# Turning the sample's 64 rows as full blocks of 128 outside the attention

## The chip, the cores and the metric

The kernel runs on one core of one Trainium2 chip. The metric is device time in microseconds (us), from the start to the end of one execution; the median of three runs of the kernel before is 1720.67 us (1717.54 to 1723.04).

## The reference, cut to what matters

One layer of a streaming encoder, for a prompt of 1024 tokens and a sample of 64 tokens with 128 cached keys, in float32. Both pass the same layer:

```python
z = rmsnorm(x, norm_mix) @ w_in                 # 1024 -> qa ka va qi ki wi qb kb vb ga gb
qa, ka, qi, ki = rmsnorm per head (not qi), rotary on the first 16 of 64 columns
qb, kb = rmsnorm per head
isc = sum_h wi[h] * relu(qi[h] @ ki.T)          # indexer: the best 256 keys (48 for the sample)
oa = softmax(qa @ ka.T / 8 over the chosen keys) @ va
ob = softmax(qb @ kb.T / 8 + bias over a band of 9 chunks) @ vb
x = x + (sigmoid(ga) * (oa @ w_o_a) + sigmoid(gb) * (ob @ w_o_b)) @ w_out
y = x + square(relu(rmsnorm(x, norm_ffn) @ w_up)) @ w_down
```

The outputs are y for prompt and sample and the new keys and values.

## The kernel before, in words

The 1024 prompt tokens are eight blocks of 128 rows (i = 0 to 7); the 64 rows of the sample are block 8 (i = NT), with rows = 64. Wherever a matmul needs tokens along the columns, a block is turned by TensorE: `nc.tensor.transpose` with the identity, four 128-column pieces of a block into one PSUM bank, then ScalarE copies the bank out rounded to float32r (the high half) and DVE subtracts that from the bank (the low half). All products are made of high and low halves by `three` (lines 154 to 156) or `two` (lines 162 and 163).

There are five places that turn a block of the sample outside the attention:

- `to_columns` (line 181), the normalised input xg, two groups of four, called by `stage_columns`;
- `index_keys` (line 241), the indexer's key kd, one transposition;
- `stage_scores` (line 349), the indexer's queries qd, two groups of four, one for each four heads;
- `rows_to_dram` (line 411), the projected t of kb, qb, ka and qa (the values vb and va are not turned), one group of four each, called by `keep` in `project_heads`;
- `ffn_columns` (line 930), the normalised input xg of the feed-forward part, two groups of four.

For i < 8 they turn 128 x 128; for the sample 64 x 128, with the identity cut to 64 x 64, and the four results stand side by side in 4 x 64 columns of the bank:

```python
nc.tensor.transpose(ps[:, q * rows:(q + 1) * rows], xg[:rows, k * P:(k + 1) * P],
                    ident[:rows, :rows])
```

The tiles come from rotating buffers: xg has 2 (line 167), kd 3, qd 2, t 3. DVE writes xg (line 172); ScalarE, DVE and POOL (rotary, lines 220 to 223, gains, line 461) write the others. POOL also makes the low halves of most weights (`split`, line 148), in whose queue everything on POOL stands in order. In the attention, `weigh_sample` (line 736) already turns the sample in full blocks.

Except in a few blocks (`issue_after`), the order of the instructions on an engine is not written by hand: the framework places them by a simulated clock, in the order in which they become ready there.

Of the kernel before, what the change touches and what calls it, by code (L numbers as in the profile page):

```python
# [44 lines left out]
def kernel(  # L45
# [58 lines left out]
    def ptile():  # L104
        return bank("pt")
# [16 lines left out]
    def copy(out, in_):  # L122
        return nc.scalar.activation(out, in_, AF.Copy)  # L123
# [42 lines left out]
    def rms_rows(pool, xt, rows, gain):  # L166
        xg = pool.tile([P, D], F32, tag="xg", name="xg", bufs=2)
        junk = pool.tile([P, D], mybir.dt.bfloat16, tag="junk", name="junk", bufs=1)
        ss = pool.tile([P, 8], F32, tag="ss", name="ss", bufs=3)
        nc.scalar.activation(junk[:rows], xt[:rows], AF.Square, accum_out=ss[:rows, 0:1])  # L170
        rs = rstd(pool, ss, D, rows, 1)
        last["scaled"] = nc.vector.scalar_tensor_tensor(xg[:rows], xt[:rows], rs[:rows, 0:1], gain[:rows],
                                                        op0=ALU.mult, op1=ALU.mult)
        return xg

    def to_columns(xg, rows, dst, c0):
        for j in range(2):
            ps = ptile()
            for q in range(4):
                k = 4 * j + q  # L180
                nc.tensor.transpose(ps[:, q * rows:(q + 1) * rows], xg[:rows, k * P:(k + 1) * P],
                                    ident[:rows, :rows])
            v = ps[:, :4 * rows].rearrange("p (q r) -> p q r", q=4)
            hi = dst[:, 4 * j:4 * j + 4, 0, c0:c0 + rows]
            last["turned"] = copy(hi, v)
            nc.vector.tensor_sub(dst[:, 4 * j:4 * j + 4, 1, c0:c0 + rows], v, hi)
# [52 lines left out]
    def index_keys(kd, rows, c0):  # L239
        ps = ptile()  # L240
        nc.tensor.transpose(ps[:, :rows], kd[:rows].rearrange("p a d -> p (a d)"), ident[:rows, :rows])
        copy(kih[:, c0:c0 + rows], ps[:, :rows])
        nc.vector.tensor_sub(kil[:, c0:c0 + rows], ps[:, :rows], kih[:, c0:c0 + rows])
# [51 lines left out]
    def stage_keys(i):  # L295
        rows = P if i < NT else TS
        z1, _ = project(i, acc(), parts["keys"], 584 - SPLIT)
        kd = ix.tile([P, 2, HD], F32, tag="kd", name="kd", bufs=3)
        ss = ix.tile([P, 8], F32, tag="ss", name="ss", bufs=3)
# [11 lines left out]
        qd = ix.tile([P, H, 2, HD], F32, tag="qd", name="qd", bufs=2)  # L311
        copy(qd[:rows, 5:8, 0, :], z1[:rows, :192].rearrange("p (h d) -> p h d", d=HD))
# [17 lines left out]
    def stage_scores(i, between={}):  # L330
# [15 lines left out]
        for j in range(2):  # L346
            ps = ptile()
            for q in range(4):
                nc.tensor.transpose(ps[:, q * rows:(q + 1) * rows],
                                    qd[:rows, 4 * j + q].rearrange("p a d -> p (a d)"), ident[:rows, :rows])  # L350
            v = ps[:, :4 * rows].rearrange("p (q r) -> p q r", q=4)
# [56 lines left out]
    def rows_to_dram(t, rows, dst, c0, gain=None):  # L408
        ps = ptile()
        for j in range(4):  # L410
            nc.tensor.transpose(ps[:, j * rows:(j + 1) * rows], t[:rows, j * P:(j + 1) * P], ident[:rows, :rows])
        v = ps[:, :4 * rows].rearrange("p (j r) -> p j r", j=4)
# [22 lines left out]
    def project_heads():  # L435
        for nm, c0, gn, roped in (("vb", C_VB, None, False), ("kb", C_KB, "kb", False), ("qb", C_QB, "qb", False),
# [9 lines left out]
            for i in range(NT + 1):  # L446
                z, rows = project(i, wide_acc(), ws, 512)
                t = pj.tile([P, 512], F32, tag="t", name="t", bufs=3)
                if gn is None:
# [469 lines left out]
    def ffn_columns(i):  # L919
# [6 lines left out]
        for j in range(2):  # L926
            ps = ptile()
            for q in range(4):
                k = 4 * j + q
                nc.tensor.transpose(ps[:, q * rows:(q + 1) * rows], xg[:rows, k * P:(k + 1) * P],  # L930
                                    ident[:rows, :rows])
            v = ps[:, :4 * rows].rearrange("p (q r) -> p q r", q=4)
# [447 lines left out]
```

## Time and profile before

| | us |
|---|---|
| median of three runs | 1720.67 (1717.54 to 1723.04) |
| the profiled execution | 1716.99 |
| its span, first to last instruction | 1715.2 |
| TensorE (PE) busy | 1693.6 |
| weight loads (PEld) busy | 1548.0 |
| DVE (VectorE) busy | 1200.7 |
| ACT (ScalarE) busy | 957.4 |
| POOL (GpSimd) busy | 454.9 |

The profile is of one execution, taken by the hardware profiler. PE is TensorE's matmul side, PEld its weight load, which runs beside it; SP issues most DMAs. In a timeline a line is one instruction, or several alike in a row (x4), with its start and duration in us, the engine, the line of the kernel, what it writes and reads, and the tile of TensorE's array as rows\*columns (64\*128 is a matmul with 64 rows of weights). Where the engine sat idle before an instruction, the bracket says how long and who ended it. Matmuls are pipelined, so the distance between two starts tells what one costs, not its recorded duration.

### The profile page before, as it was taken

To read this page: it belongs to the slowest core of one execution; us is meant where nothing else is said; L and a number is where in the kernel's file an instruction comes from. 1 tells how busy PE (TensorE), PEld (TensorE's weight loads), DVE (VectorE), ACT (ScalarE), POOL (GpSimd) and SP (SyncE) were. 2 spreads that over 40 slices of the span, in tenths; PEclk is the share of its full clock that TensorE was granted. 3 is DMA by queue.
4 is the path that set the end of the run, shared out by engine and by line. 5 is a ranking of instruction groups with operands and counts; after the bars stand their busy time and mean duration, and the time that the engine had idled before them with its cause. 6 is when DMAs were issued, how large, how long until landed. Compare 5 with 4: busy or idle time off the path is not lost. (4 is left out here: it accounts for less than half of the span.)

```text
span 1715.2 us, 30888 instructions
## 1 busy us (share of the span) xinstructions
PE 1693.6 (99%) x10552; PEld 1548.0 (90%) x10552; DVE 1200.7 (70%) x2760; ACT 957.4 (56%) x1984; POOL 454.9 (27%) x550
## 2 busy tenths in 40 slices
PE   8999999999999999999999999999999999999999
PEld 6878878778999999999999999999999978788887
DVE  6775799864957777773454446765687668877787
ACT  5784889762267777775443446544454356343430
POOL 2242441434343343342344434000000001112112
PEclk9999999999999999999999999999999999999999
DMA  5022466483488877745545459555565599565643
GB/s 176 10 77 105 147 187 172 136 267 95 138 204 204 209 170 170 171 113 161 166 146 169 158 163 297 180 175 176 176 215 192 188 304 311 173 206 150 191 127 105
DMA packets 277422, 295.01 MB, mean 172 GB/s; under 512 B 39889, under 2 KB 201937, under 8 KB 277265
## 3 DMA queue, kind: packets, MB, share of 16 engines
q1 hardware_dynamic: 248144, 257.50, 51.6%
q10 hardware_dynamic: 29120, 35.53, 5.9%
q8 instruction: 84, 1.38, 0.3%
q14 instruction: 74, 0.60, 0.1%
HBM read 199.85 MB, written 93.08 MB: 171 GB/s over the span
## 5 line engine op out<-in xcount | busy, mean ns | idle before, releaser
L155 PE MATMUL x<-lo,hi 128*128 128x512 f32 (+1 forms) x436 | 169.2, 388 | 0.3 <-DVE lo L146 0.3
L156 PE MATMUL x<-hi,lo 128*128 128x512 f32 (+1 forms) x436 | 167.6, 389 | 0.0
L154 PE MATMUL x<-hi 128*128 128x512 f32 (+1 forms) x436 | 164.9, 390 | 1.2 <-DVE q_P L1254 1.2
L148 POOL TENSOR_TENSOR lo<-wr,hi 128x512 fp32r<-128x512 f32 x12 | 31.6, 2635 | 482.7 <-ACT hi L123 482.7
L148 POOL TENSOR_TENSOR lo<-raw,hi 128x512 fp32r<-128x512 f32 x88 | 118.2, 1352 | 143.4 <-ACT hi L123 142.7
L123 ACT ACTIVATE hi<-raw 128x512 fp32r<-128x512 f32 x104 | 64.2, 626 | 90.9 <-PE acc L155 21.0
L539 ACT ACTIVATE nth<-work,cand 128x768 bf16<-128x768 f32 (+2 forms) x93 | 96.7, 1040 | 25.8 <-DVE cand L556 18.3
L155 PE MATMUL wide<-wlo,xnT 128*128 128x512 f32 x256 | 101.2, 398 | 0.0
L154 PE MATMUL wide<-whi,xnT 128*128 128x512 f32 x256 | 100.4, 398 | 0.7 <-ACT whi L123 0.7
L156 PE MATMUL wide<-whi,xnT 128*128 128x512 f32 x256 | 101.1, 397 | 0.0
L154 PEld LDWEIGHTS x<-hi 128*128 128x128 f32 x436 | 81.8, 188 | 19.0 <-DVE q_P L1254 1.6
L155 PEld LDWEIGHTS x<-lo,hi 128*128 128x128 f32 x436 | 81.9, 188 | 18.3 <-DVE lo L146 0.7
L156 PEld LDWEIGHTS x<-hi,lo 128*128 128x128 f32 x436 | 81.8, 188 | 17.8
L726 DVE TENSOR_TENSOR pl<-pt,ph 128x512 fp32r<-128x512 f32 (+2 forms) x152 | 90.9, 614 | 9.4 <-ACT ph L123 9.1
L154 PE MATMUL acc<-xnT,hi 128*128 128x384 f32 (+1 forms) x288 | 95.6, 332 | 0.0
L155 PE MATMUL acc<-xnT,hi 128*128 128x384 f32 (+1 forms) x288 | 94.5, 328 | 0.0
L156 PE MATMUL acc<-xnT,lo 128*128 128x384 f32 (+1 forms) x288 | 94.4, 328 | 0.0
L146 DVE TENSOR_TENSOR lo<-hr,hi 128x512 fp32r<-128x512 f32 x108 | 80.7, 748 | 19.4 <-ACT hi L123 19.4
L123 ACT ACTIVATE ph<-pt 128x512 fp32r<-128x512 f32 (+3 forms) x168 | 79.7, 514 | 25.3 <-PE pt L714 16.3
L701 POOL TENSOR_SCALAR mw<-mw,sm 128x640 f32<-128x640 f32 (+1 forms) x64 | 56.6, 885 | 133.8 <-DVE sm L700 131.3
L148 POOL TENSOR_TENSOR wlo<-wraw,whi 128x512 fp32r<-128x512 f32 x40 | 52.5, 1318 | 106.7 <-ACT whi L123 97.4
L123 ACT ACTIVATE hi<-wr 128x512 fp32r<-128x512 f32 x60 | 37.9, 631 | 75.5 <-issue 52.6
(679 smaller groups left out, 5999.3 us busy)
## 6 DMA issues: line engine op xcount, KB each, us to landing
hr<-h SPq DMA_DIRECT2D x108, 256.0 KB, 3.5
wr<-in_w_down_dram SPq DMA_DIRECT2D x76, 256.0 KB, 3.9
wraw<-in_w_in_dram SPq DMA_DIRECT2D x56, 256.0 KB, 2.7
h<-h ACTq DMA_DIRECT2D x32, 272.0 KB, 2.1
raw<-in_w_out_dram SPq DMA_DIRECT2D x32, 256.0 KB, 3.0
raw<-in_w_up_dram SPq DMA_DIRECT2D x32, 256.0 KB, 3.4
out_dram<-t SPq DMA_DIRECT2D x24, 256.0 KB, 2.5
g_dram<-gate SPq DMA_DIRECT2D x32, 192.0 KB, 2.8
```

The lines of the kernel that those rows point to most:

```text
L123: return nc.scalar.activation(out, in_, AF.Copy)
L146: last["lo"] = nc.vector.tensor_sub(lo, raw, hi)
L148: nc.gpsimd.tensor_sub(lo, raw, hi)
L154: nc.tensor.matmul(out, sh, mh, start=(opens and i == 0), stop=False, skip_group_check=resumes)
L155: nc.tensor.matmul(out, sh, ml, start=False, stop=False, skip_group_check=resumes)
L156: last = nc.tensor.matmul(out, sl, mh, start=False, stop=(closes and i == n - 1), skip_group_check=resumes)
L539: nc.scalar.activation(sign[:, :w.shape[1]], w, AF.Sign, bias=against, scale=-1.0, accum_out=col(cnt, j))
L701: nc.gpsimd.tensor_scalar(m[:rows, :n], m[:rows, :n], sm[:rows, 6:7], 1.0, op0=ALU.mult, op1=ALU.mult)
L726: nc.vector.tensor_sub(pl[:kr, a:b], ps[:kr, a:b], ph[:kr, a:b])
```

## The change

Each of the five places gives whole 128-row tiles to one function, `turn_rows`, which turns 128 x 128 with the full identity and hands back the first `rows` columns of each result. For the sample, the upper 64 partitions of the tile are set to zero by a memset on GpSimd (`fill`); for full blocks `fill` does nothing. There are eight such memsets: xg twice (in `rms_rows` for the first norm and again for the feed-forward part), kd, qd, and t for kb, qb, ka and qa. The evictions read the first 64 columns of every 128. The diff, cut where places repeat:

```diff
         ss = pool.tile([P, 8], F32, tag="ss", name="ss", bufs=3)
+        fill(xg, rows)
         nc.scalar.activation(junk[:rows], xt[:rows], AF.Square, accum_out=ss[:rows, 0:1])
...
+    def fill(t, rows):
+
+        if rows < P:
+            nc.gpsimd.memset(t[rows:], 0.0)
+
+    def turn_rows(srcs, rows):
+        ps = ptile()
+        for q, t in enumerate(srcs):
+            nc.tensor.transpose(ps[:, q * P:(q + 1) * P], t, ident)
+        return ps.rearrange("p (q r) -> p q r", q=4)[:, :, :rows]
+
     def to_columns(xg, rows, dst, c0):
         for j in range(2):
-            ps = ptile()
-            for q in range(4):
-                k = 4 * j + q
-                nc.tensor.transpose(ps[:, q * rows:(q + 1) * rows], xg[:rows, k * P:(k + 1) * P],
-                                    ident[:rows, :rows])
-            v = ps[:, :4 * rows].rearrange("p (q r) -> p q r", q=4)
+            v = turn_rows([xg[:, k * P:(k + 1) * P] for k in range(4 * j, 4 * j + 4)], rows)
...
     def index_keys(kd, rows, c0):
         ps = ptile()
-        nc.tensor.transpose(ps[:, :rows], kd[:rows].rearrange("p a d -> p (a d)"), ident[:rows, :rows])
+        nc.tensor.transpose(ps[:, :P], kd.rearrange("p a d -> p (a d)"), ident)
...
         kd = ix.tile([P, 2, HD], F32, tag="kd", name="kd", bufs=3)
+        fill(kd, rows)
...
         qd = ix.tile([P, H, 2, HD], F32, tag="qd", name="qd", bufs=2)
+        fill(qd, rows)
...
                 t = pj.tile([P, 512], F32, tag="t", name="t", bufs=3)
+                if nm[0] != "v":
+                    fill(t, rows)
```

`stage_scores`, `rows_to_dram` and `ffn_columns` call `turn_rows` in the same way as `to_columns` does.

## Rows read from the trace of the kernel before

**Rows 1.** The page: busy time of each engine, share of the span, instructions.

```profile
PE 1693.6 (99%) x10552; PEld 1548.0 (90%) x10552; DVE 1200.7 (70%) x2760; ACT 957.4 (56%) x1984; POOL 454.9 (27%) x550
```

**Rows 2.** Busy time by stage: stretch, length, engines' busy us, clock, DMA; first, sum.

```profile
0.00:92.00 92.00, 82.70 (x541) 72.22 (x542) 68.79 (x182) 60.69 (x152) 22.96 (x81) 0.98 0.28 87
...
960.00:1078.00 118.00, 117.41 (x979) 116.50 (x978) 65.93 (x121) 66.99 (x127) 49.45 (x35) 1.00 0.69 212
...
sum 1715.00, PE 1693.57 PEld 1547.97 DVE 1200.69 ACT 957.38 POOL 454.86; mean PE 211.70 PEld 193.50 DVE 150.09 ACT 119.67 POOL 56.86
```

**Rows 3.** Groups of TensorE by shape: count, busy us, mean ns, idle us before.

```profile
L411 PE MATMUL pt<-ident,t 64*128 64x64 f32 x16 | 1.8, 230 | 1.6 <-DVE pair L417 1.4 <-DVE cand L571 0.2
L930 PE MATMUL pt<-ident,xg 64*128 64x64 f32 x8 | 0.9, 235 | 0.0
L181 PE MATMUL pt<-ident,xg 64*128 64x64 f32 x8 | 0.9, 235 | 0.0
L349 PE MATMUL pt<-ident,qd 64*128 64x64 f32 x8 | 0.7, 228 | 0.0
...
L241 PE MATMUL pt<-ident,kd 64*128 64x64 f32 x1 | 0.2, 246 | 0.2 <-DVE qiT L354 0.2
```

**Rows 4.** Timeline of TensorE around the sample's first group at line 930.

```profile
1002.51 0.28 PE L155 MATMUL acc<-lo,mT 128*128 128x256 f32 x1
1002.72 0.46 PE L930 MATMUL pt<-ident,xg 64*128 64x64 f32 x4
1003.11 0.39 PE L156 MATMUL acc<-hi,mT 128*128 128x256 f32 x1
1003.34 0.28 PE L154 MATMUL acc<-hi,mT 128*128 128x256 f32 x1
```

**Rows 5.** Timeline of TensorE around a full block's group at line 930.

```profile
997.77 0.28 PE L154 MATMUL acc<-hi,mT 128*128 128x256 f32 x1
997.89 0.60 PE L930 MATMUL pt<-ident,xg 128*128 128x128 f32 x4
998.24 0.37 PE L155 MATMUL acc<-lo,mT 128*128 128x256 f32 x1
998.45 0.28 PE L156 MATMUL acc<-hi,mT 128*128 128x256 f32 x1
```

**Rows 6.** Timeline of TensorE: eight half transpositions, line 349; eight full ones, line 411.

```profile
116.84 0.70 PE L349 MATMUL pt<-ident,qd 64*128 64x64 f32 x8
117.48 0.44 PE L162 MATMUL s<-kih,qiT 128*128 128x384 f32 x1
...
427.56 1.04 PE L411 MATMUL pt<-ident,t 128*128 128x128 f32 x8
428.35 0.48 PE L162 MATMUL acc<-whi,xsT 128*128 128x512 f32 x1
```

**Rows 7.** Timeline of TensorE at the sample's group of kb, line 411.

```profile
243.75 0.43 PE L411 MATMUL pt<-ident,t 64*128 64x64 f32 x4 [1.43 <-DVE pair L417]
```

**Rows 8.** TensorE's waits: for whom, us in total, times, longest.

```profile
PE pt L411 <- DVE pair L417: 1.4, 1, 1.4
...
PE wide L154 <- ACT whi L123: 0.7, 1, 0.7
```

**Rows 9.** Groups of POOL by shape: memsets of 64 partitions.

```profile
L616 POOL MEMSET vhl<- 64x128 f32 x16 | 3.2, 199 | 4.1 <-PE po L744 3.3 <-PE s L162 0.9
...
L371 POOL MEMSET work<- 64x64 f32 x6 | 0.9, 148 | 12.8 <-DVE work L366 12.8
```

**Rows 10.** Timeline of all engines at a load of vhl: its two halves.

```profile
630.85 0.93 SPq L617 DMA_DIRECT2D vhl<-v_a  x1
...
631.35 0.20 POOL L616 MEMSET vhl<- 64x128 f32 x1
```

**Rows 11.** Timeline of all engines before the sample's groups at line 930.

```profile
991.76 6.11 POOL L148 TENSOR_TENSOR lo<-raw,hi 128x512 fp32r<-128x512 f32 x4 [5.45 <-ACT hi L123]
...
993.64 1.73 DVE L172 SCALAR_TENSOR_TENSOR xg<-x,rs,g_ffn 64x1024 f32<-64x1024 f32 x1 [2.33 <-PE pt L930]
```

**Rows 12.** The page's costliest groups: such a split on POOL, mean ns.

```profile
L148 POOL TENSOR_TENSOR lo<-raw,hi 128x512 fp32r<-128x512 f32 x88 | 118.2, 1352 | 143.4 <-ACT hi L123 142.7
```

More of the change, by code (lines that the diff above doesn't have):

```diff
@@ L346, in stage_scores @@
         for j in range(2):
[L347 to L351, printed above, removed]
+            v = turn_rows([qd[:, h].rearrange("p a d -> p (a d)") for h in range(4 * j, 4 * j + 4)], rows)
             dst = qiT[:, 4 * j:4 * j + 4, :rows]
@@ L408, in rows_to_dram @@
     def rows_to_dram(t, rows, dst, c0, gain=None):
[L409 to L412, printed above, removed]
+        v = turn_rows([t[:, j * P:(j + 1) * P] for j in range(4)], rows)
         both = pj.tile([P, TP], F32R, tag="pair", name="pair", bufs=3).rearrange("p (z j t) -> p z j t", z=2, j=4)
@@ L926, in ffn_columns @@
         for j in range(2):
[L927 to L932, printed above, removed]
+            v = turn_rows([xg[:, k * P:(k + 1) * P] for k in range(4 * j, 4 * j + 4)], rows)
             copy(raw[:, 4 * j:4 * j + 4, :rows], v)
```

## The prediction

> **What bounds the kernel now.** I read the busy times of the page first, then the busy time by stage, then the shapes of TensorE's instructions, and last the timeline around the transpositions that the change touches. TensorE is busy for 1693.6 of 1715.2 us [rows 1]; of the 21.4 us in which it is idle, 9.3 lie in the first 92 us [rows 2], so from there to the end 12.1 us are all that any better order could give back. The granted clock is 1.00 after the start [rows 2]: the upper of the two levels, 2.4 GHz, throughout, and nothing here rests on the clock. An edit can therefore move the time by changing what TensorE itself does, or by making it wait.
>
> The change touches one form alone, the transpositions that TensorE's records show as 64\*128. There are 41: 16 at line 411, eight each at lines 181, 349 and 930, one at line 241 [rows 3]. Their own mean, 228 to 246 ns, is longer than the distance from one to the next, since matmuls overlap, and so tells nothing of what the change is worth; the starts of the matmuls around them do.
>
> **The change part by part.**
>
> *A group of four.* Around the sample's first group at line 930, the last ordinary matmul before it starts at 1002.51 and the second after it at 1003.34: 0.83 us [rows 4]. Around a full group of four between the same 256-column matmuls these are 997.77 and 998.45: 0.68 us [rows 5]. So a group of four full transpositions takes 0.15 us less of TensorE than one of four half ones. The reason stands in the same rows: the half group begins 0.21 us after its neighbour where the full one begins after 0.12 us, and the second matmul after it follows 0.23 us after the first, against 0.21. Weights are not loaded ahead into or out of the half group. The four of the half group with their exit take 0.39 us, the full ones 0.35.
>
> *More than four.* Eight half ones, first start to the next matmul, take 117.48 − 116.84 = 0.64 us, eight full ones 428.35 − 427.56 = 0.79 us [rows 6]. Against the groups of four, the four more cost 0.25 us as halves (62 ns each) and 0.44 us as full ones (110 ns each). A full transposition is thus dearer by 48 ns; the saving is in the two ends of a group, and at line 349, where the eight stand in one piece, the change loses: 0.15 − 4 x 0.048 = −0.04 us.
>
> One rule would price that otherwise: the Trainium skill ("TensorE: Matmul & The Clock Gate", section "Back-to-back issue gap") gives 134 cycles for 128 columns and about 60 for 64 or fewer, by which the wider one would be dearer by 31 ns (an estimate at 2.4 GHz) and a group of four would save 0.22 us instead of 0.15. The rows' 48 ns decide.
>
> *The sum on TensorE.* Two groups at line 930: 0.30 us. Line 411: four groups of four, of which three begin behind a wait (the longest, 1.43 us, ends at 243.75 [rows 7]); behind a wait there is no weight load to be ahead with, so I take 0 for these (0 to 0.15 each) and 0.15 for the fourth. Line 181: 0.15 for the first group; the second is followed at once by another transposition, 0 (0 to 0.15). Line 241: a single one between waits, 0 (0 to 0.15). Line 349: −0.04. Together 0.56 us; with every zero at its upper end 1.31.
>
> *How much of it reaches the end.* What is saved before 243.75 us only lengthens the 1.43 us in which TensorE waits there for DVE, which was then working through the threshold search; so 0.26 us of it goes. The group at line 411 that saves 0.15 is followed by a wait for ScalarE of 0.7 us [rows 8], and I count it as gone too. The 0.30 us of line 930 are followed by waits as well, but in a stage in which every engine works on what TensorE has just made; I take them as kept. So: 0.30 us saved, between 0 and 1.31.
>
> *The zeros.* Eight memsets of the upper 64 partitions are added on POOL: 1024 elements a partition for the two xg tiles and for qd, 128 for kd, 512 for the t of the four heads that are turned. A memset of 64x64 takes 148 ns and one of 64x128 takes 199 [rows 9], so 0.80 ns for each further element: 0.92 us for 1024 (three), 0.51 for 512 (four), 0.20 for kd, 5.0 us together. POOL is busy for 27% of the span [rows 1]. That the written halves don't wait for one another is seen in the attention: the DMA that writes the upper 64 partitions of vhl is issued at 630.85, ahead of the memset of its lower 64 at 631.35 [rows 10]. So the memset need not hold ScalarE or DVE; it holds what is behind it in POOL's queue, and the transposition, which now waits for POOL too, and behind that all of TensorE.
>
> The tightest place is line 930. There POOL makes the low halves of the next weights, four in 6.11 us from 991.76, and the last ends at 997.87 [rows 11]; TensorE's first matmul after the group that ends at 998.24 [rows 5] uses that one, so 0.37 us are to spare. The buffer that the sample's xg takes comes free with block 2's last transposition, for which DVE waited when it begins to write it at 993.64 [rows 11], in the middle of these four. A memset put there delays TensorE by at most 0.92 − 0.37 = 0.55 us if all four splits stay as long as they are. Four at their usual 1.35 us would take 5.4 us instead of 6.11 [rows 11, 12], so some of it falls into time now lost beside DVE. I take 0.30 us; the ends are 0 and the hold worked out under the slower rival. At the other seven I take 0: POOL waits for work for long stretches around them and the splits there are ahead; the end is their 4.1 us. The evictions of the turned rows read four runs of 64 instead of one run of 256, the same element count, off TensorE's path: 0, with 0.1 us either way as bound for lack of a row.
>
> *The sum.* −0.30 + 0.30 = 0.0 us. The profiled execution took 1716.99 us, 1.79 around its span, and stays there; the median of the runs shown is 3.7 us above it at 1720.67, and the forecast is told against that: **1720.7 us**.
>
> **The rivals.**
>
> *Faster by another order.* The order of the instructions is not written by hand over most of the kernel: a framework places them by a simulated clock, in which eight new instructions and 41 wider ones can shift what follows. For it speaks that nothing pins the order outside a few blocks; against it that from 92 us on only 12.1 us of idle time are there to be won [rows 2], spread over many waits of 1.4 us and less [rows 8]. If half went, with the 0.56 us saved in full: 1720.7 − 6.6 = 1714.1 us.
>
> *Slower, by POOL's queue.* One mechanism: the memset is put ahead of weight splits and stands there until its buffer is free. At line 930, if it is first of all, POOL is held from 991.76 to 993.64, then writes for 0.92 us: the splits come 2.8 us late, 2.4 us beyond the 0.37 to spare. At line 411 the t buffer comes free only when an earlier t has been written out; if each of the four memsets holds POOL for 1 us beyond what the splits have to spare, with its own 0.51 us, that is 6.0 us. Together 8.4: 1729.1 us. It decides where the hold is longer than what the splits have to spare. For it speaks the tight place [rows 11]; against it that an order made by simulated readiness does not put an instruction where it would wait long, and that none of TensorE's longest waits is for a split of POOL [rows 8].
>
> That the change doesn't do what it says I rule out: all five places that make the 64\*128 form are in the diff.
>
> **How the numbers follow.** About 0.3% (5.2 us) is what a measurement of this kernel can tell from no change; its three runs alone lie between 1717.54 and 1723.04. The forecast, no change beyond that, has 0.79: its own bounds, −1.3 and about +2.7 us, stay within it. Faster by over 0.3% needs the first rival at nearly its full price: 0.09. Slower by over 0.3% needs the second at most of its price, or a worse order: 0.12. The range takes the scatter of the runs, 3.1 below and 2.4 above the median, and adds the bounds of the sum, 1.3 below and the 2.4 us of the hold at line 930 above: 1716.3 to 1725.5.
>
> **What would show it right or wrong.** After the change no 64\*128 form is left and 41 more full transpositions stand in TensorE's groups; around the sample's groups at line 930 the stretch reads 0.68 us instead of 0.83. The memsets read 0.9, 0.5 and 0.2 us. The three waits behind which savings vanish are still there, a little longer. TensorE's busy time falls by no more than 1.3 us. I am wrong if TensorE shows a new wait for POOL of over 1 us, at the low halves behind a memset or at a turned group; if the memset of qd or t delays ScalarE's write of the lower half; or if the stages behind 1078 us, which the change does not touch, become longer or shorter by microseconds through another order.

## The result, and the profile after

The kernel after takes 1731.36 us (median of six runs, 1727.55 to 1736.49), the kernel before beside it 1719.87 us (six runs, 1717.54 to 1723.04): a ratio of 1.0071, 95% interval [1.0057, 1.0086]. It is slower by 0.7%, some 11 us, and lies above the whole predicted range. The profiled execution took 1727.55 us with a span of 1725.8, so 10.6 us more span than the one of before; that difference is what the trace has to explain.

The page's busy times, which answer to [rows 1]:

```profile
PE 1695.3 (98%) x10552; PEld 1549.8 (90%) x10552; DVE 1207.8 (70%) x2760; ACT 956.9 (55%) x1984; POOL 458.2 (27%) x558
```

TensorE is busy 1.7 us longer, though the change was to save it 0.6; the rest of the 10.6 us is time in which it waits. DVE is busy 7.1 us longer although it has as many instructions as before. POOL has its eight memsets more and is busy 3.3 us longer.

The two things that the change itself does came out as they were priced. POOL's groups by shape hold the memsets (count, busy us, mean ns):

```profile
L180 POOL MEMSET t<- 64x512 f32 x4 | 2.1, 522 | 1.2 <-POOL wlo L148 1.0
L180 POOL MEMSET xg<- 64x1024 f32 x2 | 1.9, 948 | 0.1
L180 POOL MEMSET qd<- 64x1024 f32 x1 | 1.0, 987 | 0.6 <-PE pt L185 0.6
...
L180 POOL MEMSET kd<- 64x128 f32 x1 | 0.2, 201 | 1.5 <-issue 1.5
```

And TensorE's timeline around the sample's group in the feed-forward part, now four full transpositions (all turns have line 185):

```profile
1012.29 0.28 PE L155 MATMUL acc<-lo,mT 128*128 128x256 f32 x1
1012.41 0.60 PE L185 MATMUL pt<-ident,xg 128*128 128x128 f32 x4
1012.77 0.37 PE L156 MATMUL acc<-hi,mT 128*128 128x256 f32 x1
1012.97 0.28 PE L154 MATMUL acc<-hi,mT 128*128 128x256 f32 x1
```

1012.97 − 1012.29 = 0.68 us, where the half group took 0.83 [rows 4]. So the loss is not in what was changed. Cutting the span at the stages (first matmul of the heads, of the attention, and so on; busy time of PE, PEld, DVE, ACT, POOL, then clock and DMA) finds it. The heads stage, in which the projections of the heads and the threshold search run side by side (DVE and ScalarE find, one bit a step, the score that the chosen keys must reach), after:

```profile
163.20:489.40 326.20, 316.74 (x1512) 263.75 (x1511) 260.42 (x704) 202.47 (x394) 119.59 (x147) 0.99 0.53 157
```

The same stage before:

```profile
163.00:480.00 317.00, 314.68 (x1511) 262.56 (x1510) 250.90 (x702) 202.29 (x394) 120.58 (x143) 1.00 0.54 160
```

Of the 10.6 us, 9.2 are lost between 163 and 489 us: TensorE is idle there for 9.5 us instead of 2.3, and busy for 2.1 us longer. The stages behind it differ by 1.3 us and less (the up product most, 343.2 against 341.9). The whole of DVE's excess stands there too (260.42 against 250.90). TensorE's waits in this stage (us in total, times, longest):

```profile
PE pt L185 <- DVE pair L419: 5.0, 2, 4.2
PE pt L185 <- POOL t L230: 2.1, 1, 2.1
PE wide L155 <- DVE wlo L146: 1.2, 1, 1.2
PE pt L185 <- POOL t L465: 0.9, 1, 0.9
```

Before, the longest wait of this kind was the 1.43 us of [rows 7]. The 4.2 us are the piece to follow. They stand in TensorE's timeline:

```profile
243.48 0.40 PE L155 MATMUL wide<-wlo,xnT 128*128 128x512 f32 x1
248.05 1.09 PE L185 MATMUL pt<-ident,t 128*128 128x128 f32 x4 [4.17 <-DVE pair L419]
248.79 0.78 PE L156 MATMUL wide<-whi,xnT 128*128 128x512 f32 x1
```

and they are dearer than they look, as the windows around them show (the first pair of numbers in a row is TensorE's busy time, the first after the engines the granted clock):

```profile
240.00:244.00 4.00, 2.94 (x14) 1.81 (x12) 3.84 (x5) 0.81 (x3) 3.13 (x4) 1.00 0.59 191
244.00:248.00 4.00, 0.00 (x0) 0.00 (x0) 3.83 (x9) 2.73 (x6) 1.14 (x1) 0.97 0.08 25
248.00:252.00 4.00, 3.95 (x13) 3.37 (x14) 2.41 (x8) 3.25 (x7) 1.27 (x1) 0.60 0.86 222
```

TensorE does nothing from 244 to 248, and in the 4 us after that the granted clock averages 0.60, mostly its lower level (0.5, 1.2 GHz): 4 x (1 − 0.60) = 1.6 us more. That is most of the 2.1 us by which it is busy longer. So this place costs 4.17 − 1.43 + 1.6 = 4.3 us, about half of the 9.2; the rest is the other waits of the list, which no run here follows one by one.

What did TensorE wait for? The group is the sample's, in kb. The turned groups take two banks by turns, so it goes into the bank of kb's block 6, which was turned at 235.61 and is emptied in two steps, ScalarE's copy and DVE's subtraction at line 419. That subtraction comes only at 247.21, 11.6 us after the turn (before: turned at 234.51, subtracted at 242.92, 8.4 us). DVE's timeline up to it:

```profile
239.38 1.17 DVE L139 TENSOR_TENSOR nt<-nt,ms 64x8 f32<-64x8 f32 x1
240.58 1.20 DVE L140 SCALAR_TENSOR_TENSOR rs<-nt,r 64x8 f32<-64x8 f32 x1
...
242.67 1.35 DVE L568 COPY_PREDICATED bits<-ok,cand 128x6 int32<-128x6 int32 x1
244.05 1.12 DVE L560 TENSOR_SCALAR cand<-bits 128x6 int32<-128x6 int32 x1
...
247.21 0.69 DVE L419 TENSOR_TENSOR pair<-pt,pair 128x512 fp32r<-128x512 f32 x1
```

DVE is not idle; four operations on six or eight elements a partition take 4.84 us in front of the subtraction, where others of their kind take 0.15 to 0.17 each. ScalarE's copy is late too, behind a search step that waits for the last of the four:

```profile
246.20 0.57 ACT L123 ACTIVATE pair<-pt 128x512 fp32r<-128x512 f32 x1
```

POOL's timeline in the same stretch says why:

```profile
239.24 1.29 POOL L148 TENSOR_TENSOR wlo<-wraw,whi 128x512 fp32r<-128x512 f32 x1 [3.12 <-ACT whi L123]
240.49 1.27 POOL L465 TENSOR_TENSOR t<-t,g_kb 128x512 f32<-128x512 f32 x1
242.64 1.29 POOL L465 TENSOR_TENSOR t<-t,g_kb 64x512 f32<-64x512 f32 x1 [0.87 <-DVE ok L567]
243.89 1.25 POOL L148 TENSOR_TENSOR wlo<-wraw,whi 128x512 fp32r<-128x512 f32 x1
```

Each long operation of DVE begins just after one of POOL and ends with it: 239.38 + 1.17 = 240.55 against 240.53, 240.58 + 1.20 = 241.78 against 241.76. In the kernel before, DVE has two such operations between the same turn and the same subtraction, 2.49 us instead of 4.84:

```profile
237.68 1.26 DVE L563 TENSOR_TENSOR ok<-cnt,lim 128x6 int32<-128x6 f32 x1
...
238.97 1.23 DVE L564 COPY_PREDICATED bits<-ok,cand 128x6 int32<-128x6 int32 x1
...
242.92 0.69 DVE L417 TENSOR_TENSOR pair<-pt,pair 128x512 fp32r<-128x512 f32 x1
```

The instructions are the same; their order is not. Compared engine by engine, the two programs differ in about 50 places on ScalarE, 53 on DVE and 22 on POOL (eight of these the new memsets). On ScalarE and DVE most of them lie between the point where the sample's qd is turned and the end of the heads stage; in the attention and in the last stage there are none. So the theory: **the longer transpositions shift the simulated clock, it places the rest in another order, and in that order more of DVE's small operations meet POOL's.** (Over the whole heads stage 31 small operations of DVE last over 0.4 us, and 28 in the kernel before.) The rivals: the work itself (wider turns in TensorE's queue, zeros in POOL's), or one of the five places.

### The profile page after: what moved, and what is told of

Same layout as the page of the kernel before. It is cut to its first block, busy times and chain, and to the rows that moved or that the text cites. A ratio compares the mean times of both kernels' runs of the same rounds, so it can differ in the third digit from the quotient of the medians.

```text
span 1725.8 us, 30897 instructions
## 1 busy us (share of the span) xinstructions
PE 1695.3 (98%) x10552; PEld 1549.8 (90%) x10552; DVE 1207.8 (70%) x2760; ACT 956.9 (55%) x1984; POOL 458.2 (27%) x558
## 4 chain that ended last, share of the span: by engine, by line
PE 70%; DMA 3%; DVE 2%; issue 2%; POOL 1%; ACT 1%; SPq 0%; ACTq 0%; POOLq 0%; DVEq 0%
PE acc L154 6%; PE acc L155 6%; PE acc L156 6%; PE x L156 5%; PE x L155 5%; PE x L154 5%; PE pt L718 3%; PE po L734 2%; PE s L162 2%; PE pe L156 2%; PE pg L156 2%; PE pe L154 2%; PE pe L155 2%; PE pg L154 2%; PE pg L155 2%; PE s L163 2%
## 5 line engine op out<-in xcount | busy, mean ns | idle before, releaser
L148 POOL TENSOR_TENSOR lo<-wr,hi 128x512 fp32r<-128x512 f32 x12 | 25.9, 2160 | 485.1 <-ACT hi L123 485.1
L123 ACT ACTIVATE hi<-raw 128x512 fp32r<-128x512 f32 x104 | 64.2, 626 | 96.5 <-PE acc L155 20.8
L543 ACT ACTIVATE nth<-work,cand 128x768 bf16<-128x768 f32 (+2 forms) x93 | 96.7, 1040 | 27.2 <-DVE cand L560 20.8
L146 DVE TENSOR_TENSOR lo<-hr,hi 128x512 fp32r<-128x512 f32 x108 | 80.5, 747 | 20.9 <-ACT hi L123 20.8
```

Source lines behind the costliest of these rows:

```text
L146: last["lo"] = nc.vector.tensor_sub(lo, raw, hi)
L148: nc.gpsimd.tensor_sub(lo, raw, hi)
L543: nc.scalar.activation(sign[:, :w.shape[1]], w, AF.Sign, bias=against, scale=-1.0, accum_out=col(cnt, j))
```

## The experiments

"Heads stage" is the stretch from its first matmul to the first of the attention (before 317.0 us with 2.3 us of TensorE idle, after 326.2 and 9.5); "wait" is TensorE's wait ahead of the sample's group of kb, at 243 to 254 us (before 1.43, after 4.17). All ratios are to the kernel before on the same chip.

| run | us | ratio [95%] | heads stage, idle | wait |
|---|---|---|---|---|
| e1 zeros alone | 1721.78 | 1.0013 [0.9999, 1.0026] | 317.8, 1.8 | 1.82 |
| e2 heads alone | 1724.21 | 1.0029 [1.0015, 1.0043] | 318.7, 4.1 | 1.77 |
| e3 indexer alone | 1723.96 | 1.0028 [1.0015, 1.0041] | 322.0, 4.0 | 2.72 |
| e4 feed-forward alone | 1719.15 | 0.9998 [0.9982, 1.0013] | 317.8, 1.9 | 1.72 |
| e5 queries twice | 1727.11 | 1.0033 [1.0021, 1.0046] | 322.2, 4.0 | 2.70 |
| e6 full rows, old order | 1721.83 | 1.0011 [0.9998, 1.0023] | 317.6, 1.7 | 1.74 |
| e7 all but queries | 1726.88 | 1.0036 [1.0018, 1.0054] | 322.7, 6.1 | 1.96 |
| e8 all twice | 1727.27 | 1.0039 [1.0027, 1.0050] | 323.9, 4.6 | 2.66 |
| e9 change and six more | 1725.83 | 1.0030 [1.0016, 1.0044] | 320.1, 4.0 | 2.00 |
| e10 one step pinned | 1733.68 | 1.0091 [1.0075, 1.0108] | 327.6, 9.1 | 4.17 |
| e11 half rows, late order | 1727.54 | 1.0055 [1.0039, 1.0071] | 325.6, 7.3 | 2.59 |
| e12 change and eight more | 1732.27 | 1.0077 [1.0061, 1.0092] | 329.2, 9.0 | 2.77 |
| e13 eviction first | 1731.06 | 1.0058 [1.0046, 1.0071] | 324.3, 7.6 | 1.08 |
| e14 gains on DVE | 1725.53 | 1.0027 [1.0013, 1.0042] | 319.6, 2.8 | none |
| e15 before, gains on DVE | 1722.73 | 1.0010 [0.9999, 1.0020] | 318.2, 2.3 | none |

### One part at a time (e1 to e4)

Four kernels do one part of the change each. e1 has all eight memsets, but turns half rows. e2 to e4 turn full rows, with their zeros, in one part: the projected heads (`rows_to_dram`); the first norm, the key and the queries of the indexer (`to_columns`, `index_keys`, `stage_scores`); and the feed-forward part. The other places keep the old turn:

```diff
+    def turn_half(srcs, rows):
+        ps = ptile()
+        for q, t in enumerate(srcs):
+            nc.tensor.transpose(ps[:, q * rows:(q + 1) * rows], t[:rows], ident[:rows, :rows])
+        return ps[:, :4 * rows].rearrange("p (q r) -> p q r", q=4)
```

> The eight memsets are there, every transposition stays at 64 rows. Laid beside the kernel before, the static order of the engines' queues is all but the same (18 places differ on TensorE, 7 on DVE, against 63 and 53 in the changed kernel). Order theory (the 11.5 us come from another order of the queues between 160 and 470 us): within 0.2% of before, 1717 to 1723 us, TensorE idle about 18 to 20 us, threshold search 188 us from first to last step. Zeros theory (the memsets in POOL's queue hold the splits or the turned groups): slower by 6 us or more, with new waits of TensorE for POOL.

> Only the groups of kb, qb, ka and qa are turned as 128 rows, with their four memsets; the other places stay as before. Place theory (the loss is made directly at the turned groups of the heads, where TensorE waits 4.2 and 2.1 us in the changed kernel): slower by 6 to 11 us, with these waits in it. Order theory: the order differs from before in 70 places but little is moved (312 TensorE rows against 1406), so the time is nearer to before than to the changed kernel: slower by 0 to 5 us, search 187 to 192 us.

> Only the sample's turns before 120 us (xg of the first norm, kd, qd) are of 128 rows, with their three memsets; the groups of the heads and of the feed-forward part stay as before. Place theory and zeros theory: no loss, within 0.2% of before, since what stands in the heads is what stood there before. Order theory: the order of the queues behind them is that of the changed kernel more than that of before (1360 TensorE rows moved against before, 475 against the changed one), so slower by 5 to 12 us, between 160 and 470 us, where this kernel executes the same instructions as before.

> Only the feed-forward part's two groups are of 128 rows, with one memset. All theories: within 0.2% of before. By the prediction's own sum 0.3 us less on TensorE in the two groups (0.68 us instead of 0.83 around each) and up to 0.6 us of a later split.

The zeros alone and the feed-forward part alone can't be told from no change (their intervals include 1). The heads and the indexer cost 0.29% and 0.28%, as ratios to the kernel before. Their sum, 0.57%, is less than the 0.71% of the whole, but the more telling point is where e3 loses. Its edits are done by 163 us, before the heads stage begins, and still its heads stage is 5.0 us longer than before, with the same kind of wait (TensorE's waits, e3):

```profile
PE pt L192 <- DVE pair L426: 3.4, 2, 2.7
```

Work that was over 80 us earlier can't hold an eviction at 245 us; its shadow on the order can. (In time e3 lost 4.6 us, a little under the 5 to 12 expected.) Most of the 5.0 us is the clock behind the wait: TensorE is busy for 318.0 us in that stage instead of 314.7, and idle for 1.7 us more. e2 loses in another way: its heads stage is only 1.7 us longer, and in its profiled execution the attention (354.6 us, before 351.3) and the last stage (346.2, before 343.0) are longer too; more of that below.

### The same shift without the change (e5, e8), the change without the shift (e6, e7)

e5 is the kernel before with each of the sample's eight half transpositions of qd done twice: no zeros, no full rows. Through the heads stage its instructions stand in the order of e3 on ScalarE and on DVE, one by one.

```diff
-                nc.tensor.transpose(ps[:, q * rows:(q + 1) * rows],
-                                    qd[:rows, 4 * j + q].rearrange("p a d -> p (a d)"), ident[:rows, :rows])
+                for _ in range(1 if i < NT else 2):
+                    nc.tensor.transpose(ps[:, q * rows:(q + 1) * rows],
+                                        qd[:rows, 4 * j + q].rearrange("p a d -> p (a d)"), ident[:rows, :rows])
```

e8 doubles the sample's transpositions at all five places in this way. e6 is the whole change without the queries and the projected heads, the two parts that move most of the order; e7 is without the queries alone:

```diff
-        fill(qd, rows)
...
-            v = turn_rows([qd[:, h].rearrange("p a d -> p (a d)") for h in range(4 * j, 4 * j + 4)], rows)
+            v = turn_half([qd[:, h].rearrange("p a d -> p (a d)") for h in range(4 * j, 4 * j + 4)], rows)
```

> The kernel before, with the sample's eight half transpositions of the indexer's queries made twice (8 more of 62 ns; no zeros, no full rows anywhere). The queues of ACT, DVE and POOL come out in the order of the run with the indexer's turns alone, but for its three memsets. Order theory: slower by 2 to 7 us as that run was (0.28%), lost between 220 and 490 us. A theory in which full rows or zeros themselves cost: at most the 0.5 us that the eight repeats take on TensorE, within 0.1% of before.

> Full rows and zeros for xg of the first norm, kd and xg of the feed-forward part; the queries and the heads are turned as before. The order of the queues stays nearly that of before (9 places differ on TensorE, 7 on DVE). Order theory: within 0.15% of before, and by the prediction's sum up to 0.5 us faster. Theory that full rows or zeros cost: slower by 0.2% or more.

> The changed kernel with the queries alone turned as before: 33 of the 41 transpositions are full and seven of the eight memsets are there. Its order is nearer to before (422 TensorE rows moved) than to the changed kernel (1179). Order theory: slower by 2 to 7 us, like the run with the heads alone, not by 11. If instead the loss goes with the number of full transpositions and zeros: slower by 8 to 11 us.

> The kernel before, with all 41 half transpositions of the sample made twice (41 more of 62 ns, 2.5 us of TensorE if all counted; no zeros, no full rows). The order of ACT, DVE and POOL in the heads is near that of the changed kernel (82 ACT rows and 193 DVE rows differ, against 301 and 398 from before). Order theory: slower by 5 to 14 us, of which at most 2.5 us are the repeats, with waits of TensorE of over 2 us at turned groups between 220 and 370 us. Otherwise: slower by 2.5 us at most.

e5 is as slow as e3, and its heads stage agrees within 0.2 us (322.2 and 322.0), as do its waits (e5):

```profile
PE pt L412 <- DVE pair L418: 3.7, 2, 2.7
```

So what e3 loses needs neither zeros nor full rows. e6, with zeros and full rows in the first norm, the key and the feed-forward part but nearly the old order, has the heads stage of before (317.6) and a ratio whose interval includes 1. e7 and e8 are each in another order again and lose 0.36% and 0.39%. None of the eight, though, showed the 4.17 us, and no sum of parts gave it.

Over the whole table the order sorts the runs. In e1, e4 and e6 ScalarE and DVE have the order of before through the whole heads stage, and all three intervals include 1. In the kernel after and the twelve other runs they have another order there, with the change or without it, and all are slower with an interval above 1 but e15, whose interval includes 1.

### Other orders (e9, e11, e12) and one step pinned (e10)

The next four aim at the place itself. In the changed kernel ScalarE's copy of kb's block 6, the first step of the eviction that TensorE waits for, stands behind a search step that stood behind it before. (The expectations call it block 7's; by the trace it is block 6's, block 7's comes next.) e9 and e12 are the whole change plus three or four transpositions of the identity, not read by anything, ahead of each of the sample's two groups of qd; with three, ScalarE falls back into the old order at that place. e11 goes the other way: the kernel before plus three such half transpositions ahead of each of the sample's groups of qd and t, by which it falls into the changed kernel's order at that place. e10 is the whole change with the counts of that search step issued behind the eviction of block 7, and so behind that of block 6; the small operations ahead of the counts are not pinned.

The kernel after with three (e9) or four (e12) more:

```diff
+            for _ in range(3 if rows < P else 0):
+                nc.tensor.transpose(ptile()[:, :P], ident, ident)
             v = turn_rows([qd[:, h].rearrange("p a d -> p (a d)") for h in range(4 * j, 4 * j + 4)], rows)
```

The kernel before with three more, here and in the same way in `rows_to_dram` (e11):

```diff
+            for q in range(3 if rows < P else 0):
+                nc.tensor.transpose(ps[:, :TS], ident[:TS], ident[:TS, :TS])
             for q in range(4):
                 nc.tensor.transpose(ps[:, q * rows:(q + 1) * rows],
```

The kernel after with a pin in the search (e10), where `evicted` holds the two steps of each eviction:

```diff
+PIN = {19: 7}
...
+            with ExitStack() as order:
+                for ins in evicted[PIN[b]] if b in PIN else ():
+                    order.enter_context(tc.issue_after(ins.ins))
```

> The whole change, and three more transpositions of the identity ahead of each of the sample's two groups of qd (their results are not read), so more work on TensorE than the changed kernel has: 6 x about 0.11 us. They shift the simulated clock, and on ScalarE the copy of kb's block 7 out of the turned bank again stands ahead of the next two search steps, as in the kernel before, where the changed kernel has it behind them. Order theory: the 4.17 us wait at 248 us is gone (under 2 us there), the heads stage is back from 326.2 us to 317 to 320, and the time is below that of the changed kernel, 1720 to 1724 (ratio to before 1.000 to 1.002; no more than 1.003 if another place of this order is worse). Rival, the work itself (full rows, memsets): the loss stays, 1731 or more (ratio 1.007 to 1.008).

> The whole change, and one search step (bit 19) issued behind the copy and the subtraction of kb's block 7, so that ScalarE's queue has that copy ahead of the search step that held it. Nothing is added to or taken from the work. Order theory: the wait at 248 us falls from 4.17 to under 2 us with no fall of the clock behind it, the time falls by 3 to 6 us against the changed kernel, to 1725 to 1728 (ratio 1.003 to 1.005), if the orders further on, which shift too, are as good as those they replace; they may take it back or add to it by about 3 us. Rival, the work itself: 1731 (1.007) as in the changed kernel.

> The kernel before, with half rows and without zeros, and three more half transpositions of the identity ahead of each of the sample's groups of qd and t (18, about 1.1 us of TensorE; their results are overwritten). By the shifted simulated clock ScalarE has the copy of kb's block 7 behind two search steps, the same local order as in the changed kernel. Order theory: the wait at about 245 to 250 us is 3 us or more, the heads stage 322 to 327 us, the time 1726 to 1732 (ratio 1.003 to 1.007). Rival, the work itself: only the 1.1 us added, 1721 to 1722 (ratio up to 1.001), with a wait of about 1.4 us there.

> As the run with six more, with four more for each group of qd instead of three (eight, about 0.9 us): one step further, and the scheduler falls into yet another order, in which ScalarE has the copy of kb's block 7 behind one search step. Order theory: a time that does not go by the work: anywhere between 1719 and 1732 (ratio 0.999 to 1.007), other than that of the run with six more by over 2 us though only 0.2 us of work lies between them, with the difference in the heads stage. Rival, the work itself: 0.2 us more than the run with six more, whatever that is.

Three of the four speak for the order, plainly. e9 has more work than the changed kernel and is faster, 1.0030 against 1.0071 with intervals that don't touch; its heads stage is 6.1 us shorter. It does not come back all the way: 1725.83 us where 1720 to 1724 was expected, and a heads stage of 320.1 us where 317 to 320 was. e12 has 0.2 us more work than e9 and is 6.4 us slower, with a heads stage 9.1 us longer. And e11, without a zero or a full row, loses 0.55%, with 8.6 us of it in the heads stage; its wait at the place is 2.59 us, short of the 3 expected, but three more at other groups make up for it (e11's waits):

```profile
PE pt L413 <- DVE pair L421: 3.4, 2, 2.6
PE pt L415 <- DVE pair L421: 2.9, 3, 1.4
```

e10 missed. ScalarE's copy of block 6 now stands ahead of the search step and is done at 242.44 instead of 246.77, and the wait is the same to 0.01 us. Timelines of ScalarE, TensorE, DVE and POOL in e10:

```profile
241.87 0.57 ACT L124 ACTIVATE pair<-pt 128x512 fp32r<-128x512 f32 x1
```

```profile
248.25 1.09 PE L186 MATMUL pt<-ident,t 128*128 128x128 f32 x4 [4.17 <-DVE pair L421]
```

```profile
243.81 1.33 DVE L574 COPY_PREDICATED bits<-ok,cand 128x6 int32<-128x6 int32 x1
245.18 2.34 DVE L563 TENSOR_SCALAR cand<-bits 128x6 int32<-128x6 int32 x1
247.43 1.28 DVE L421 TENSOR_TENSOR pair<-pt,pair 128x512 fp32r<-128x512 f32 x2
```

```profile
243.78 1.26 POOL L468 TENSOR_TENSOR t<-t,g_kb 64x512 f32<-64x512 f32 x1 [0.87 <-DVE ok L573]
245.00 2.48 POOL L149 TENSOR_TENSOR wlo<-wraw,whi 128x512 fp32r<-128x512 f32 x2
```

An earlier copy did not help, since DVE's subtraction (here of blocks 6 and 7 at once) stands in DVE's queue behind the same small operations. One of them, an OR on six numbers a partition, now takes 2.34 us, through two of POOL's splits. That part of the theory, the place on ScalarE, fell, and what was left was DVE's queue and POOL.

### DVE's queue and POOL (e13 to e15)

e13 is the whole change with the sample's norm of kb put behind the subtraction of block 7 on DVE, and so behind that of block 6:

```diff
-                    rs = rstd(pj, ss, HD, rows, 8)
+                    with tc.issue_after(last["pair"].ins) if (nm, i) == ("kb", NT) else ExitStack():
+                        rs = rstd(pj, ss, HD, rows, 8)
```

e14 is the whole change with kb's nine gain multiplications on DVE instead of POOL, and e15 makes the same move in the kernel before:

```diff
-                        nc.gpsimd.tensor_mul(tv, tv, gains[gn][:rows, None, :].to_broadcast([rows, 8, HD]))
+                        (nc.vector if nm == "kb" else nc.gpsimd).tensor_mul(tv, tv, gains[gn][:rows, None, :].to_broadcast([rows, 8, HD]))
```

> The whole change, and on DVE the sample's norm of kb (its five small operations) issued behind the subtraction that evicts kb's block 7; nothing is added to or taken from the work. In the changed kernel, and in the run with one search step pinned, that subtraction stands behind them and behind the search step's small operations, of which four last 1.1 to 2.3 us beside POOL's gains and low halves. Theory (DVE's queue, lengthened by POOL, makes the wait): TensorE's wait for block 7's group falls from 4.17 us to under 2 us, and the heads stage gets 2 to 5 us shorter than the changed kernel's 326.2; the time 1725 to 1729 (ratio 1.003 to 1.006), if orders further on do not take it back. The sample's own group may wait longer than it did, up to 2 us. Rival (the wait belongs to the work or to ScalarE): the wait stays at about 4 us and the time at 1731 or more.

> The whole change, with the nine multiplications by kb's gain done on DVE instead of POOL (1.27 us each there, about 0.7 on DVE). Theory (POOL's operations hold DVE's small ones): between 205 and 252 us fewer of DVE's small operations last over 0.4 us, and in the heads stage their lengthening falls from 26.8 us to 18 to 23; the wait of 4.17 us at 248 us falls under 2.5 us; DVE gets 6 us more work and the order shifts again, so the time is anywhere from 1721 to 1731 (ratio 1.001 to 1.007), more likely below the changed kernel. Rival (POOL has no part in it): the lengthening stays at 25 us or more, and the time at 1731 or, for DVE's 6 us more, above.

> The kernel before, half rows and no zeros, with kb's gain on DVE as in the run before this. If POOL's hold on DVE costs more than the order it falls into, it is faster than before: 1715 to 1719 (ratio 0.997 to 0.9995), the heads stage under 317 us, lengthening 13 to 17 us instead of 19.7. If the lottery of the order decides, 1719 to 1730 (ratio 1.000 to 1.006) whatever the lengthening says.

e13 took the 4.17 us away: block 6's subtraction now runs at 244.62, block 7's at 249.58, and the sample's group (in one piece with the next) waits 1.08 us, for POOL (TensorE, e13):

```profile
253.62 1.09 PE L185 MATMUL pt<-ident,t 128*128 128x128 f32 x8 [1.08 <-POOL t L466]
```

But the heads stage got only 1.9 us shorter (2 to 5 expected), because the rest of the order moved too and put shorter waits elsewhere (e13's waits, heads stage):

```profile
PE pt L185 <- DVE pair L419: 3.2, 3, 1.8
PE wide L154 <- ACT whi L123: 1.9, 3, 0.9
PE pt L185 <- POOL t L466: 1.8, 2, 1.1
```

The time, 1731.06, is above the 1725 to 1729 expected; as a ratio, 1.0058, it is within.

e14 is the clearest. With the gains off POOL, DVE has about 6 us more to do, and yet its small operations lose 16.4 us beside POOL in the heads stage, not 26.8 (the excess over the median of their kind, where it is over 0.3 us; 19.7 us before, 21.1 in e13, 28.4 in e10). The waits for evictions are all but gone, the stage is back to 319.6 us, and what is left in it is small (e14's waits, heads stage):

```profile
PE wide L154 <- ACT whi L123: 1.1, 1, 1.1
PE pt L185 <- POOL t L230: 0.6, 1, 0.6
PE pt L185 <- DVE pair L419: 0.4, 1, 0.4
```

The place itself can be read in all the traces: how long DVE's small operations of over 0.4 us last, taken together, between the turn of block 6 and its subtraction, and how long the sample's group then waits for that subtraction. It is 2.5 to 2.6 us in the kernel before, e1, e2, e4, e6, e7 and e9 (waits of 1.4 to 2.0 us), 3.6 in e3, e5, e8 and e11 (2.6 to 2.7) and 4.84 in the kernel after (4.17); e12 (3.0, and 2.77) and e10 (6.0, and 4.17) stand a little off this line. In e13 it is 2.4, and the group no longer waits for that subtraction; in e14 it is none and in e15 1.28, and neither waits. So POOL's hold on DVE is the mechanism of the wait that was followed.

It is not shown to be all that an order costs. The sum over the stage does not go by the time: e3 and e5 lose 5 us in the heads stage with 20.8 and 21.5 us of it, hardly more than before. e15, in the kernel before, lowers it to 16.8 us, and the time is the same or 0.1% up, which by its expectation speaks for the order and not for the sum. And in e14 the order shifts as well; no run here parts the two. No kernel here beats the one before.

**What stays open.** e2, e7, e10, e12, e13 and e14 lose more in their profiled execution than their heads stages explain. Their attention takes 353.6 to 355.8 us (before 351.3). The excess stands in its first microseconds, in one wait for the attention's first weights m, which POOL scales, with the lower clock behind it (e14's waits):

```profile
PE pt L718 <- POOL m L705: 2.8, 1, 2.8
```

It is 1.6 to 3.0 us in these six, 0.9 before and 1.3 after. In e14, by the profile, POOL's m is late because ScalarE sits idle for 3.9 us ahead of a copy into gate, until an earlier gate has been written out (2.5 us before). The last stage takes 343.4 to 349.3 us in these six (before 343.0); in e13, where it is longest, the excess is one wait and the clock behind it (e13's waits):

```profile
PE x L154 <- DVE q_P L1254: 3.6, 1, 3.6
```

This wait is 1.2 us in the profile of before, 3.4 to 3.6 in those of e5, e7, e11, e12, e13 and e14, and missing from those of the changed kernel and of e9. Both of these are the fastest of their kernel's runs, which spread over 1727.55 to 1736.49 and 1720.07 to 1730.09. The order in these stages does not decide either wait: in the attention and in the last stage the instructions of TensorE, ScalarE, DVE and POOL stand in the same order in all these kernels. What does, the arrival of transfers or what the heads stage leaves behind, was not tried, and with one profile for each kernel it is not known how many of its executions have them. Nor was it settled whether the 0.1% of e1 and e6 is real.

## Why the prediction was wrong

**The range and the likeliest case were wrong:** 1720.7 us, 1716.3 to 1725.5, with 0.12 for what happened.

- *TensorE's own saving.* Right where it can be read: the group of the feed-forward part (line 930 before) takes 0.68 us as forecast. (A slip that changes no sum: of the 0.26 us that "goes", 0.11 are saved before 243.75 us; the 0.15 of the fourth group at line 411, added in the next sentence, is in the 0.26 already.) But TensorE's busy time was to fall by up to 1.3 us and rose by 1.7, because of the lower clock behind the new wait. "Nothing here rests on the clock" held for the kernel before only.
- *The zeros.* Right: 0.95 to 0.99, 0.52 and 0.20 us, and by e1 no measurable cost. The memset of the feed-forward part stands between two pairs of splits and holds up nothing; TensorE has no new wait there.
- *The rival of POOL's queue.* It gave 1729.1 us, close to the truth, by a mechanism that did not happen: TensorE has no new wait for a split of POOL. The agreement of the number is chance. (The upper bound of the sum took only the 2.4 us of line 930 and left out the 4.1 us given as the end of the other seven memsets; with them the range would have ended near 1729.6, still below the result.) Two waits for POOL of 0.9 and 2.1 us came at turned groups, the second over the 1 us in the list of what would prove me wrong, but for a gain and a rotary addition put in another order.
- *The step that failed* is the treatment of the order. The prediction saw that "eight new instructions and 41 wider ones can shift what follows" and made of it only "faster by another order", bounded by the 12.1 us of idle time that a better one could give back. A worse order was three words, "or a worse order", inside another rival's chance: no mechanism, no price, and 0 in the sum. The bound works in one direction only. In its place the runs showed a worse order in the heads stage: 9.2 us more there, of which TensorE waits 7.1 us longer (9.46 us idle instead of 2.32) and is busy 2.1 us longer. With 12.1 us of idle time left after the start, an order drawn anew had little to win and much to lose, and e5, e9, e11 and e12 show the sizes: ratios of 1.003 to 1.008 for edits that add 0.5 to 2 us of work or less.
- *The rows that could have told.* The wait of [rows 7], 1.43 us for the subtraction, was read as a place where savings vanish. It was also the place with the least room: one more POOL operation beside DVE there is 1.2 us more wait. [Rows 11] shows four splits at 6.11 us where four would take 5.4 at their usual length [rows 12], which was put down to "time now lost beside DVE"; the other side of that, DVE's own loss, was not looked up.
- *The issue gap.* By the estimate from the Trainium skill's figures ("TensorE: Matmul & The Clock Gate", section "Back-to-back issue gap") the group of four would have saved 0.22 us; 0.83 − 0.68 = 0.15 is what it saves. Neither touches the outcome.

## What to carry to other kernels

Where a framework places instructions by a simulated clock, price every edit that changes a modelled duration as a fresh draw of the order, two-sided, and look up how far the present order is from its bound: here 2.3 us idle in 317, so that nearly every draw was a loss, up to 0.9%. A dummy edit that adds half a microsecond of unread work in the same place (e5, e9) shows the size of such draws for the price of a run, and should come before any theory of the real edit. And where POOL and DVE work side by side, count DVE's small operations on the path, not its elements: each can cost a whole POOL operation.

## What the runs showed of the hardware

A small operation of DVE that begins while POOL works on a `tensor_tensor` is mostly held until that one ends. In the heads stage of the changed kernel 31 operations on at most eight elements a partition (reads of accumulators not counted) last over 0.4 us. All 31 run beside a POOL operation, and 30 of them end 20 to 33 ns after it does. Operations with two inputs from SBUF, the predicated copy and the one-input `tensor_scalar` are all among them. Of 211 such operations with no POOL operation beside them none lasts over 0.4 us. Another 55 overlap one of POOL and stay short, and most of these fit: 21 begin less than 0.4 us before POOL's operation ends and also end 20 to 31 ns after it; 19 begin at its very end and outlast it by more; 8 begin before POOL's does and are not held. Seven run through the midst of one: five `tensor_scalar` on one element a partition, and a reciprocal and a predicated copy beside a memset. The Trainium skill ("SBUF — State Buffer", section "SBUF: two separate sides") states that DVE and GpSimd share a pair of ports by an exclusive lock: whichever starts first holds it for the whole instruction, on DVE's side for operations with two inputs from SBUF (against a GpSimd operation that reads SBUF) or in a mode that uses both ports. This trace agrees, with 0.15 us against 1.1 to 1.35, and 2.34 and 2.52 us (e12's predicated copy at 242.71) where two POOL operations follow each other.

A single idle stretch of TensorE was followed by the lower clock: 4.17 us idle, then a mean of 0.60 over 4 us (after); in e13's last stage 3.6 us idle, then

```profile
1488.00:1492.00 4.00, 0.89 (x2) 0.80 (x3) 4.00 (x8) 0.00 (x0) 0.00 (x0) 0.76 0.73 222
1492.00:1496.00 4.00, 4.00 (x11) 3.04 (x11) 4.00 (x6) 2.30 (x4) 1.29 (x1) 0.50 0.11 37
1496.00:1500.00 4.00, 4.00 (x17) 3.28 (x16) 3.11 (x6) 1.16 (x2) 0.00 (x0) 0.89 0.78 238
```

that is 0.50 for 4 us and 0.89 for the next four: 4 x 0.50 + 4 x 0.11 = 2.4 us on top of the 3.6. The 1.43 us wait of [rows 7] was not followed by it: from 230 to 260 us the granted clock of the kernel before is 1.00, where that of the changed one is 0.94 (before, then after):

```profile
230.00:260.00 30.00, 28.57 (x136) 22.91 (x135) 27.81 (x95) 25.35 (x52) 8.89 (x7) 1.00 0.73 200
230.00:260.00 30.00, 24.74 (x107) 19.29 (x107) 27.60 (x73) 21.53 (x45) 10.49 (x9) 0.94 0.56 159
```

The length of the wait alone does not decide it. In the same stretch e4, with a wait of 1.72 us, has 0.94; e2 and e7, with 1.77 and 1.96, have 1.00; and e3 and e5, with 2.7, have 0.89, a dearer fall than the changed kernel's behind 4.17.
